# Attention logits as whole-array one-pass products: query parts stacked on the rows, keys doubled and split

## The chip, the core and the metric

The kernel runs on one core of a Trainium2 chip. A core has a matrix engine (TensorE, PE in the profile, with its weight loads shown apart as PEld), a vector engine (VectorE, DVE), a scalar engine with activation functions (ScalarE, ACT), a general engine (GpSimd, POOL) and a queue that issues transfers (SyncE, SP). Each works through its own instructions in order; they wait for one another by semaphores. The metric is the device time of one execution in microseconds, as the median of several.

## What is computed

Two layers of a sequence encoder on 512 tokens of width 1024. Layer 0 mixes tokens by differential attention, layer 1 by gated linear attention; both also attend to 256 memory tokens and end with a gated MLP. The change touches the differential attention of layer 0: six heads, each with two maps of logits (m = 0, 1) of width 64.

```
q = rms_norm(q, qk_norm_g[0]) * (d ** -0.5)        # d = 64
k = rms_norm(k, qk_norm_g[1])
...
logits = einsum('bhmqd,bhmkd->bhmqk', qb, k) + bias
logits = where(visible, logits, -inf)               # chunks of 64 tokens
p = softmax(logits, axis=-1)
w = p[:, :, 0] - lam * p[:, :, 1]
o = einsum('bhqk,bhkv->bhqv', w, v)
```

The heads' outputs are normalised, put beside the memory attention's and sent through the output projection.

## The kernel before

**Number formats.** Everything is held in 32 bits. A product of two F32 operands is issued by `mm` as two records in the profile. Where that is to be avoided, an operand is split into a part `hi`, rounded to the shorter format F32R, and the rest `lo`, also F32R; the large products are sums of three F32R products (hi hi, hi lo, lo hi: L249 to L251 for token-major results, L266 to L268 for feature-major ones). `split` (L231) makes `hi` on ACT and `lo` on DVE; `split_weights` (L198) does so for weights, piece by piece, as they arrive from memory.

**Order.** TensorE runs its instructions exactly as they are written (`manual_schedule`); the other engines' instructions are ordered by the framework when the program is built. So that TensorE has something to do while a softmax is on its way, the independent projections stand in a list, `Filler` (L88): each unit has a cost in us (a quarter of a 128-token block of a projection, six matmuls, counts 6 x 512 / 2370 = 1.296; a unit of output projection, three matmuls, 0.65), and `F.fill(us)` emits units until its credit is used. `F.need(name)` emits all up to a mark.

**Layer 0** (`diff_layer`, L543). The first projection of queries and keys (for heads 0 and 1) is computed at the start; `norms` normalises each 64-column group of the queries, then of the keys (`group_norm`, L298: squares on ACT, sums on DVE, a reciprocal root with one Newton step, a multiplication of 1024 columns on DVE). Then the projection for values and memory queries goes into the filler list, `F.fill(10.0)` emits eight units of it, and `prepare(0)`, one more unit, `prepare(1)` follow. `prepare(h)` (L570) turns the head's 128 columns of queries (both maps) with four TensorE transposes into a PSUM bank, evacuates them on ACT with the gain, and does the same for the keys; so map 0 lies on rows 0 to 63 and map 1 on rows 64 to 127.

A loop of 28 steps follows. Step t emits: `logits(t)` for block t of 24 (head t // 4, 128 queries, 128 (t % 4 + 1) keys); `values(t - 2)`; a fill; at t = 5, 6, 13, 14 `norms` of the next pair of heads (queries at 5 and 13, keys at 6 and 14); `turn(t - 1)`, which transposes the softmax weights; a slot of the memory attention (from t = 12; it turns and multiplies its own blocks); a second fill; at t = 7, 8, 15, 16 `prepare` of heads 2, 3, 4, 5; at t = 7, 11, 15, ... `finish`, which turns a finished head and splits it for the output projection. The fills are 3.0 us each up to t = 13 and 1.2 us after. The filler holds the projections of heads 2 and 3, the memory keys of layer 0, the values, the projection of heads 4 and 5, the memory keys of layer 1, and from t = 14, 20 and 24 on three parts of the output projection (16, 16 and 8 units). What is left is flushed behind the loop; then the last part of the output projection runs.

`logits(u)` (L586) takes two banks of the PSUM ring `lg`, one per map, and for each of two halves of the keys issues one F32 product per map, on 64 rows each. PSUM has four rings of two banks: `mm`, `sm`, `lg` and `tp`; every transpose goes to `tp`, the memory attention's logits to `lg` too.

Of the kernel before, what the change touches and what calls it, by code (L numbers as in the profile page):

```python
# [9 lines left out]
F32 = mybir.dt.float32  # L10
# [117 lines left out]
def trunk(ctx, tc, x_t, mem_t, wpack, cols_a_d, cols_d, conv_d, gate_d, rel_bias, diff_lambda, consts, onehot, out):  # L128
# [169 lines left out]
    def group_norm(pool, y, nb, ng, d, on_dve=False):  # L298
        ss = small("ss")
        for b in range(0, nb, 2):  # L300
            sq = xtile()[:, :2 * ng * d]
            A.activation(sq, y[:, b:b + 2].rearrange("p b n -> p (b n)"), AF.Square)
            V.reduce_sum(ss[:, b * ng:(b + 2) * ng], sq.rearrange("p (g d) -> p g d", d=d), axis=AX.X)
        r = rsqrt(ss[:, :nb * ng], nb * ng, 1.0 / d, on_dve)
        yv = y.rearrange("p b (g d) -> p (b g) d", d=d)
        V.tensor_mul(yv, yv, r.unsqueeze(2).to_broadcast([128, nb * ng, d]))
# [122 lines left out]
    def mem_kv(l):  # L429
# [27 lines left out]
        F.add(0.0, lambda: group_norm(None, km[0], 2, 4, 64))  # L457
# [4 lines left out]
    class MemAttn:  # L462
# [4 lines left out]
        def norm(self):  # L467
            group_norm(self.pool, self.qm, NB, 4, 64, self.on_dve)
# [74 lines left out]
    def diff_layer(pool, mix):  # L543
# [13 lines left out]

        def project_qk(pr):
            qk[pr] = (pool.tile([128, NB, 256], F32, name="qs", bufs=1),
                      pool.tile([128, NB, 256], F32, name="ks", bufs=1))  # L560
            gemm(xh, xl, NB, ("qk", pr), 512, halves(*qk[pr]))
# [8 lines left out]
        def prepare(h):  # L570
            pr, j = divmod(h, 2)
            t2 = []
            for src, g, nm in zip(qk[pr], (c_dq, c_dk), ("qT", "kT")):
                dst = pool.tile([128, S], F32, name=nm, bufs=3)
                p = bank("tp")
                for b in range(NB):
                    transpose(p[:, blk(b)], src[:, b, blk(j)])
                A.activation(dst, p, AF.Copy, scale=g)
                t2.append(dst)
            sm = cp.tile([128, 16], F32, name="smd", tag="smd")  # L580
            heads[h] = dict(q=t2[0], k=t2[1], s2=sm.rearrange("p (m b) -> p m b", b=8),
                            nm=small("nmd"), rc=small("rcd"), v=vs[pr], j=j)
# [3 lines left out]
        def logits(u):  # L586
# [11 lines left out]
            cuts = (0, nk) if i == 0 else (0, nk // 2, nk)  # L598
            for k0, k1 in zip(cuts, cuts[1:]):
                for m in range(2):  # L600
                    hh = blk(m, 64)
                    mm(pls[m][:, k0:k1], H["q"][hh, blk(i)], H["k"][hh, k0:k1], start=True, stop=True)
# [27 lines left out]
        def values(u):  # L630
# [8 lines left out]
            if i == 3:  # L639
# [5 lines left out]
                group_norm(pool, o, NB, 1, 128)  # L645

        def finish(h):
            p = bank("tp")
            for b in range(NB):
# [5 lines left out]
        qk[0] = (pool.tile([128, NB, 256], F32, name="qs", bufs=1),  # L655
                 pool.tile([128, NB, 256], F32, name="ks", bufs=1))
        ev = halves(*qk[0])
# [6 lines left out]
        F.fill(10.0)  # L664
        prepare(0)
        F.fill(1.2)
        prepare(1)
        ma = MemAttn(pool, 0, qm, mix, False)
        M0 = 12
        for t in range(28):  # L670
# [37 lines left out]
            if t in (7, 8, 15, 16):  # L708
                prepare(2 * (t // 7) + (t + 1) % 8)
# [5 lines left out]
    def gla_layer(pool, mix, acc):  # L715
# [199 lines left out]
        for h in range(4):  # L915
# [16 lines left out]
            group_norm(pool, o_[h], NB, 1, 192, True)  # L932
# [204 lines left out]
```

## Time and profile before

| | |
|---|---|
| median of 3 runs | 1207.43 us (1206.88 to 1207.71) |
| the profiled execution | 1206.7 us |
| its span, first to last instruction | 1204.9 us |
| mean granted TensorE clock | 1.000 |
| layer 0's loop, logits first to last | 44.1 to 227.3 us |

In the profile, a line such as `L602 PE MATMUL ps_lg<-kT,qT 64*128 64x128 f32 x72 | 8.4, 308 | ...` is a group of instructions: source line, engine, operation, what is written from what, shape of the weights and of the operand, count, busy time in us and mean of one in ns, and then the idle time of the engine just before them with what ended it. F32R operands are shown as f32 on PE and as fp32r where ACT and DVE write them. A line of the timeline begins with its start and its length in us; several equal instructions in a row are one line with a count. A busy share of TensorE counts pipelined matmuls, so what a matmul costs is read from the distance between starts.

### The profile page before, as it was taken

How to read it: one execution, taken by the hardware profiler on the slowest of the kernel's cores; microseconds unless marked ns; L12 is line 12 of the kernel's file. 1: busy time of each engine (PE TensorE's matmuls, PEld its weight loads, DVE VectorE, ACT ScalarE, POOL GpSimd, SP SyncE). 2: the span in 40 equal slices, each digit the busy share in tenths (PEclk: the TensorE clock that was granted, in tenths of full speed). 3: DMA queues.
4: the chain of work that ended last, by engine and by line, in shares of the span. 5: the costliest groups of instructions: out<-in, count | busy, mean ns of one | idle time of the engine just before them, and what ended most of it. 6: DMA issues, size and time to landing. Idle time of an engine off the chain costs nothing.

```text
span 1204.9 us, 14764 instructions
## 1 busy us (share of the span) xinstructions
PE 1191.4 (99%) x5678; PEld 974.2 (81%) x5678; DVE 758.8 (63%) x1257; ACT 539.7 (45%) x913; POOL 22.9 (2%) x35
## 2 busy tenths in 40 slices
PE   9999999999999999999999999999999999999998
PEld 6887877778888888888787888987888888888887
DVE  7566578887776434767546446768777653476741
ACT  6666666554444222434436444436444432243420
POOL 0000000000000000000110000003000000000000
PEclk9999999999999999999999999999999999999999
DMA  8322231232332331322341221133223233142231
GB/s 291 123 96 80 79 123 45 70 108 85 104 106 70 123 105 57 135 71 88 124 153 59 70 70 58 60 129 128 83 93 117 70 122 93 67 125 83 88 114 44
DMA packets 39376, 117.74 MB, mean 98 GB/s; under 512 B 4685, under 2 KB 5732, under 8 KB 39306
## 3 DMA queue, kind: packets, MB, share of 16 engines
q1 hardware_dynamic: 39162, 116.79, 30.0%
q8 instruction: 44, 0.72, 0.2%
q14 instruction: 26, 0.21, 0.1%
q10 hardware_dynamic: 144, 0.02, 0.0%
HBM read 112.58 MB, written 4.21 MB: 97 GB/s over the span
## 4 chain that ended last, share of the span: by engine, by line
PE 92%; DVE 4%; ACT 2%; issue 1%; DMA 1%; ACTq 0%; DVEq 0%
PE ps_mm L266 8%; PE ps_mm L267 8%; PE ps_mm L268 8%; PE ps_sm L266 6%; PE ps_sm L267 6%; PE ps_sm L268 6%; PE ps_mm L249 6%; PE ps_mm L251 6%; PE ps_mm L250 6%; PE ps_tp L266 3%; PE ps_tp L267 3%; PE ps_tp L268 3%; PE ps_lg L267 3%; PE ps_lg L268 3%; PE ps_lg L266 3%; PE ps_tp L168 2%
## 5 line engine op out<-in xcount | busy, mean ns | idle before, releaser
L199 ACT CAST whi<-raw 128x1024 fp32r<-128x1024 f32 (+4 forms) x215 | 208.4, 974 | 246.7 <-PE ps_tp L267 133.8
L200 DVE TENSOR_TENSOR wlo<-raw,whi 128x1024 fp32r<-128x1024 f32 (+4 forms) x215 | 241.5, 1133 | 110.4 <-ACT whi L199 109.4
L266 PE MATMUL ps_mm<-xsh,whi 128*128 128x512 f32 x480 | 190.7, 397 | 2.0 <-DVE xt L950 2.0
L267 PE MATMUL ps_mm<-xsl,whi 128*128 128x512 f32 x480 | 187.1, 390 | 0.1
L268 PE MATMUL ps_mm<-xsh,wlo 128*128 128x512 f32 x480 | 187.1, 390 | 0.0
L249 PE MATMUL ps_mm<-whi,xsh 128*128 128x512 f32 (+2 forms) x352 | 138.6, 394 | 0.0
L266 PE MATMUL ps_sm<-xsh,whi 128*128 128x512 f32 x352 | 136.9, 389 | 0.0
L267 PE MATMUL ps_sm<-xsl,whi 128*128 128x512 f32 x352 | 136.9, 389 | 0.0
L268 PE MATMUL ps_sm<-xsh,wlo 128*128 128x512 f32 x352 | 136.9, 389 | 0.0
L251 PE MATMUL ps_mm<-whi,xsl 128*128 128x512 f32 (+2 forms) x352 | 131.3, 373 | 0.3 <-DVE xsl L233 0.3
L250 PE MATMUL ps_mm<-wlo,xsh 128*128 128x512 f32 (+2 forms) x352 | 130.6, 371 | 0.0
L999 ACT ACTIVATE cvo<-u,cv 128x512 f32<-128x512 f32 x88 | 71.6, 814 | 113.9 <-DVE u L997 113.5
L266 PEld LDWEIGHTS ps_mm<-xsh,whi 128*128 128x128 f32 x480 | 90.2, 188 | 22.2 <-DVE xt L950 2.4
L268 PEld LDWEIGHTS ps_mm<-xsh,wlo 128*128 128x128 f32 x480 | 90.1, 188 | 19.1
L267 PEld LDWEIGHTS ps_mm<-xsl,whi 128*128 128x128 f32 x480 | 90.2, 188 | 18.8 <-DVE xsl L233 0.8
L1000 DVE SCALAR_TENSOR_TENSOR cvo<-u,cv,cvo 128x512 f32<-128x512 f32 x88 | 65.9, 749 | 31.6 <-ACT cvo L999 31.4
L249 PEld LDWEIGHTS ps_mm<-whi,xsh 128*128 128x128 f32 x352 | 66.3, 188 | 13.8 <-issue 3.2
L268 PEld LDWEIGHTS ps_sm<-xsh,wlo 128*128 128x128 f32 x352 | 66.1, 188 | 13.8
L266 PEld LDWEIGHTS ps_sm<-xsh,whi 128*128 128x128 f32 x352 | 66.1, 188 | 13.7
L267 PEld LDWEIGHTS ps_sm<-xsl,whi 128*128 128x128 f32 x352 | 66.1, 188 | 13.6
L251 PEld LDWEIGHTS ps_mm<-whi,xsl 128*128 128x128 f32 x352 | 66.1, 188 | 12.7 <-DVE xsl L233 0.5
L250 PEld LDWEIGHTS ps_mm<-wlo,xsh 128*128 128x128 f32 x352 | 66.5, 189 | 9.3
(238 smaller groups left out, 1766.9 us busy)
## 6 DMA issues: line engine op xcount, KB each, us to landing
raw<-in_wpack_dram SPq DMA_DIRECT2D x176, 512.0 KB, 3.6
raw<-in_wpack_dram SPq DMA_DIRECT2D x28, 256.0 KB, 2.8
xt<-in_x_t_dram SPq DMA_DIRECT2D x16, 256.0 KB, 4.9
xres<-xt SPq DMA_DIRECT2D x8, 256.0 KB, 2.0
xt<-xres SPq DMA_DIRECT2D x8, 256.0 KB, 3.7
out_dram<-xt SPq DMA_DIRECT2D x8, 256.0 KB, 2.0
bt<-bias_d SPq DMA_DIRECT2D x6, 256.0 KB, 5.5
raw<-in_wpack_dram SPq DMA_DIRECT2D x4, 384.0 KB, 2.9
```

What stands on the lines that cost most here:

```text
L168: nc.tensor.transpose(dst, src, ident[:n, :n])
L199: A.copy(hi[:, c], raw[:, c])
L200: V.tensor_sub(lo[:, c], raw[:, c], hi[:, c].bitcast(F32))
L249: mm(p, sh[k][:, blk(b)], hi, start=k == 0, stop=False)
L250: mm(p, sh[k][:, blk(b)], lo, start=False, stop=False)
L251: mm(p, sl[k][:, blk(b)], hi, start=False, stop=k == KT - 1)
L266: mm(p, hi[:, blk(n)], bh, start=i == first, stop=False)
L267: mm(p, hi[:, blk(n)], bl, start=False, stop=False)
L268: mm(p, lo[:, blk(n)], bh, start=False, stop=i == last)
L999: A.activation(c, u[:, 2:], AF.Identity, scale=cv[l][:, 2, j:j + 1], bias=cv[l][:, 3, j:j + 1])
L1000: V.scalar_tensor_tensor(c, u[:, 1:S + 1], cv[l][:, 1, j:j + 1], c, op0=ALU.mult, op1=ALU.add)
```

## The change

Queries and keys are held with room for two copies of each 64-column group: `doubles()` makes tiles of [128, 4, 4, 2, 64]. After the norm the queries' second copy becomes their value rounded to F32R (ACT) and the first the rest (a subtraction on DVE); the keys' second copy is a plain copy (ACT). A transposed map then has 128 rows: 64 of the queries' rest and 64 of the rounded queries, and the keys twice. Both gains go to the keys (`c_dk` is multiplied by `c_dq` once). `prepare(h, m)` works on one map: four transposes and a copy of the queries into F32R, four transposes of the keys and a split into `kh` and `kl`. `logits` issues, per map, one F32R product with `kh` and one with `kl` over all keys, 128 rows deep, into the same bank.

The order changes with it: 12.5 us of filler instead of 10 ahead of the first preparation, a fill of 1.2 behind each of the four preparations there, and in the loop the first map is prepared ahead of `turn`, the second where the head was prepared before. `group_norm` takes its groups as one dimension, which is only another way of writing it for most callers; for the memory keys it makes two halves of 256 columns instead of one of 512.

```diff
-    def group_norm(pool, y, nb, ng, d, on_dve=False):
+    def group_norm(y, d, on_dve=False):
+        n = y.shape[1]
         ss = small("ss")
...
+        for h in (slice(0, n // 2), slice(n // 2, n)):
+            sq = xtile()[:, :n // 2 * d].rearrange("p (g d) -> p g d", d=d)
+            A.activation(sq, y[:, h], AF.Square)
+            V.reduce_sum(ss[:, h], sq, axis=AX.X)
+        r = rsqrt(ss[:, :n], n, 1.0 / d, on_dve)
+        V.tensor_mul(y, y, r.unsqueeze(2).to_broadcast([128, n, d]))
...
+        V.tensor_mul(c_dk, c_dk, c_dq)
...
+        def doubles():
+            return [pool.tile([128, NB, 4, 2, 64], F32, name=n, bufs=1) for n in ("qs", "ks")]
+
+        def ev_qk(q, k):
+            def ev(b, p):
+                for d, c in ((q, p[:, :256]), (k, p[:, 256:])):
+                    A.activation(d[:, b, :, 0], c.rearrange("p (g d) -> p g d", d=64), AF.Copy, scale=r[:, b:b + 1])
+            return ev
...
         def norms(pr, i):
             F.need(f"qk{pr}")
-            group_norm(pool, qk[pr][i], NB, 4, 64)
+            y = qk[pr][i].rearrange("p b g t d -> p (b g) t d")
+            group_norm(y[:, :, 0], 64)
+            if i:
+                A.copy(y[:, :, 1], y[:, :, 0])
+            else:
+                A.copy(y[:, :, 1].bitcast(F32R), y[:, :, 0])
+                V.tensor_sub(y[:, :, 0], y[:, :, 0], y[:, :, 1])
...
+        def prepare(h, m):
             pr, j = divmod(h, 2)
...
+            q, k = (t[:, :, 2 * j + m].rearrange("p b t d -> p b (t d)") for t in qk[pr])
+            p = bank("tp")
+            for b in range(NB):
+                transpose(p[:, blk(b)], q[:, b])
+            H["q", m] = pool.tile([128, S], F32R, name=f"qT{m}", bufs=2)
+            A.copy(H["q", m], p)
+            p = bank("tp")
+            for b in range(NB):
+                transpose(p[:, blk(b)], k[:, b])
+            H["kh", m] = pool.tile([128, S], F32R, name=f"kh{m}", bufs=2)
+            H["kl", m] = pool.tile([128, S], F32R, name=f"kl{m}", bufs=2)
+            split(H["kh", m], H["kl", m], p, c_dk)
...
-            cuts = (0, nk) if i == 0 else (0, nk // 2, nk)
-            for k0, k1 in zip(cuts, cuts[1:]):
-                for m in range(2):
-                    hh = blk(m, 64)
-                    mm(pls[m][:, k0:k1], H["q"][hh, blk(i)], H["k"][hh, k0:k1], start=True, stop=True)
+            for m in range(2):
+                for part in ("kh", "kl"):
+                    mm(pls[m][:, :nk], H["q", m][:, blk(i)], H[part, m][:, :nk], start=part == "kh",
+                       stop=part == "kl")
...
-        F.fill(10.0)
-        prepare(0)
-        F.fill(1.2)
-        prepare(1)
+        F.fill(12.5)
+        for h in range(2):
+            for m in range(2):
+                prepare(h, m)
+                F.fill(1.2)
...
+            ahead = 2 * (t // 7) + (t + 1) % 8 if t in (7, 8, 15, 16) else None
+            if ahead:
+                prepare(ahead, 0)
             if 0 <= t - 1 < 24:
                 turn(t - 1)
             ma.slot(t - M0)
             F.fill(f)
-            if t in (7, 8, 15, 16):
-                prepare(2 * (t // 7) + (t + 1) % 8)
+            if ahead:
+                prepare(ahead, 1)
```

More of the change, by code (lines that the diff above doesn't have):

```diff
@@ L295, in trunk, with groups @@
     c_go = lambda t: col(23 + t)
-    def group_norm(pool, y, nb, ng, d, on_dve=False):
+    def group_norm(y, d, on_dve=False):
+        n = y.shape[1]
         ss = small("ss")
[L300 to L306, printed above, removed]
+        for h in (slice(0, n // 2), slice(n // 2, n)):
[4 more added lines that the diff above has]
+        V.tensor_mul(y, y, r.unsqueeze(2).to_broadcast([128, n, d]))
+    def groups(y, d):
+        return y.rearrange("p b (g d) -> p (b g) d", d=d)
     def bias_rows(rb, oh, bs):
@@ L567, in norms @@
             F.need(f"qk{pr}")
-            group_norm(pool, qk[pr][i], NB, 4, 64)
-        def prepare(h):
-            pr, j = divmod(h, 2)
[L572 to L582, printed above, removed]
+            y = qk[pr][i].rearrange("p b g t d -> p (b g) t d")
[6 more added lines that the diff above has]
+        def prepare(h, m):
+            pr, j = divmod(h, 2)
+            if m == 0:
+                sm = cp.tile([128, 16], F32, name="smd", tag="smd")
+                heads[h] = dict(s2=sm.rearrange("p (m b) -> p m b", b=8), nm=small("nmd"), rc=small("rcd"),
+                                v=vs[pr], j=j)
+            H = heads[h]
+            q, k = (t[:, :, 2 * j + m].rearrange("p b t d -> p b (t d)") for t in qk[pr])
[10 more added lines that the diff above has]
+            split(H["kh", m], H["kl", m], p, c_dk)
         live = {}
```

18 lines of the change are left out of this document (8 added, 10 removed).

## The prediction

> **What bounds the kernel now.** I read the page's busy shares and chain of waits first, then busy time by stretch, then TensorE instruction by instruction.
>
> ```profile
> PE 1191.4 (99%) x5678; PEld 974.2 (81%) x5678; DVE 758.8 (63%) x1257; ACT 539.7 (45%) x913; POOL 22.9 (2%) x35
> ...
> PE 92%; DVE 4%; ACT 2%; issue 1%; DMA 1%; ACTq 0%; DVEq 0%
> ```
>
> ```profile
> 44.00:215.00 171.00, 167.58 (x942) 133.70 (x941) 118.34 (x316) 109.43 (x276) 0.58 (x4) 1.00 0.28 87
> 215.00:260.00 45.00, 43.13 (x227) 34.00 (x226) 38.65 (x79) 23.79 (x48) 0.20 (x4) 1.00 0.26 82
> ```
>
> The columns after the length are PE, PEld, DVE, ACT and POOL busy time, the granted clock, DMA share and GB/s. TensorE is the bound throughout, in a fixed order, so time changes by what its own stream loses or gains and by each place where it waits. In the stretch that the change touches (44 to 215 us) DVE is busy 69% and ACT 64%: room on average, none to be sure of at a given moment.
>
> The logits (L602) are issued as f32 products on 64 rows, each as two records:
>
> ```profile
> L602 PE MATMUL ps_lg<-kT,qT 64*128 64x128 f32 x72 | 8.4, 308 | 1.0 <-ACT kmT L454 0.6 <-ACT xt L492 0.3
> ...
> L602 PE MATMUL ps_lg<-kT,qT 64*128 64x256 f32 x48 | 8.2, 406 | 0.6 <-ACT xt L492 0.5
> ```
>
> Busy time hides their price; the order of starts shows it. Three blocks, for 256, 512 and 128 keys, with what stands around them:
>
> ```profile
> 51.21 0.39 PE L251 MATMUL ps_mm<-whi,xsl 128*128 128x512 f32 x1
> 51.52 0.72 PE L602 MATMUL ps_lg<-kT,qT 64*128 64x128 f32 x8
> 52.17 0.50 PE L249 MATMUL ps_mm<-whi,xsh 128*128 128x512 f32 x1
> 52.51 0.39 PE L250 MATMUL ps_mm<-wlo,xsh 128*128 128x512 f32 x1
> ...
> 66.07 0.39 PE L251 MATMUL ps_mm<-whi,xsl 128*128 128x512 f32 x1
> 66.39 1.14 PE L602 MATMUL ps_lg<-kT,qT 64*128 64x256 f32 x8
> 67.45 0.71 PE L638 MATMUL ps_sm<-v,xt 128*128 128x128 f32 x4
> 67.92 0.48 PE L249 MATMUL ps_mm<-whi,xsh 128*128 128x512 f32 x1
> 68.23 0.39 PE L250 MATMUL ps_mm<-wlo,xsh 128*128 128x512 f32 x1
> 68.47 0.40 PE L251 MATMUL ps_mm<-whi,xsl 128*128 128x512 f32 x1
> ...
> 74.97 0.39 PE L251 MATMUL ps_mm<-whi,xsl 128*128 128x512 f32 x1
> 75.29 0.49 PE L602 MATMUL ps_lg<-kT,qT 64*128 64x128 f32 x4
> 75.71 0.94 PE L638 MATMUL ps_sm<-v,xt 128*128 128x128 f32 x6
> 76.72 0.39 PE L250 MATMUL ps_mm<-wlo,xsh 128*128 128x512 f32 x1
> ```
>
> Undisturbed projection products start 0.23 us apart (68.23, then 68.47). So 256 keys cost 52.51 - 51.21 - 2 x 0.23 = 0.84 us of the stream. With the value products (L638) taken out at 0.11 us each (the row of eight in the last fence: 1.05 us, less one 0.27 us tail, over seven), 512 keys cost 2.16 - 0.46 - 0.44 = 1.26, 128 keys 1.75 - 0.46 - 0.67 = 0.62. That is 0.21 us per 128 keys and 0.41 us whatever the size; 384 keys, on the same line, cost 1.05. The 0.41 lies before and behind the block (0.31 from L251 to L602 instead of 0.23, 0.34 from L249 to L250), and the f32 value products, on all 128 rows, show none of it: it belongs to going to half the rows and back.
>
> **The change part by part.** *Products (A).* Four one-pass products per block, 128 rows deep, replace them. Priced as the projections' products, 512 keys take 4 x 0.23 = 0.91. A width of 256 is in the trace, in the second layer:
>
> ```profile
> 772.62 0.28 PE L249 MATMUL ps_mm<-whi,xsh 128*128 128x256 f32 x1
> 772.74 0.28 PE L250 MATMUL ps_mm<-wlo,xsh 128*128 128x256 f32 x1
> ```
>
> 0.12 us each: 0.48 for 256 keys, and 0.70 for 384 by the line between. One-pass products 128 wide don't occur. The lower end is the same line carried on (0.065 each); the upper is the old rate, 0.21. I take 0.11, that of the nearest rows of this width (value products and transposes), since a weight load goes with each: 0.45. A head then costs 0.45 + 0.48 + 0.70 + 0.91 = 2.54 instead of 0.62 + 0.84 + 1.05 + 1.26 = 3.77; six heads save 7.4 us. [...]
>
> Against that stand transposes: sixteen a head for eight, 48 more. Four of q and then four of k:
>
> ```profile
> 180.38 0.60 PE L168 MATMUL ps_tp<-C,qs 128*128 128x128 f32 x4
> 180.81 0.60 PE L168 MATMUL ps_tp<-C,ks 128*128 128x128 f32 x4
> 181.84 0.66 PE L168 MATMUL ps_tp<-C,o 128*128 128x128 f32 x4 [0.42 <-ACT qT L578]
> ```
>
> 180.38 to 180.81 is four: 0.108 each, 5.2 us. **A = -2.2 us** (-3.3 to +0.2 by the ends of the 128-wide price).
>
> *ACT and DVE.* The durations:
>
> ```profile
> L199 ACT CAST whi<-raw 128x1024 fp32r<-128x1024 f32 x19 | 20.0, 1051 | 4.5 <-PE ps_mm L251 4.1 <-DMA raw<-in_wpack_dram 0.4
> ...
> L578 ACT ACTIVATE kT<-ps_tp,cols 128x512 f32<-128x512 f32 x6 | 4.1, 687 | 0.0
> ...
> L627 ACT COPY xt<-ps_tp 128x512 f32<-128x512 f32 x4 | 2.3, 581 | 0.0
> ```
>
> ```profile
> L306 DVE TENSOR_TENSOR qs<-qs,rs_y 128x1024 f32<-128x1024 f32 x2 | 2.5, 1225 | 0.1
> ...
> L233 DVE SCALAR_TENSOR_TENSOR xsl<-ps_tp,cols,xsh 128x512 fp32r<-128x512 f32 x3 | 2.3, 751 | 10.8 <-ACT xsh L232 10.8
> ```
>
> ACT: six copies of 1024 columns (6.3 us), and twelve q copies (0.58) plus twelve upper key parts (0.69) instead of twelve at 0.69: +13.3 us. DVE: three subtractions of 1024 (3.7) and twelve lower key parts (9.0): +12.7 us. Over 171 us ACT goes to 72% and DVE to 77%. Under TensorE's stream that is free; it costs where TensorE stands right behind it. The strided evacuations keep their element counts, and I cost them, the 64-column halves of the memory keys' norm and the one tiny product of gains at nothing: all lie under projections; uncovered they are under 0.5 us together.
>
> *Transpose banks (D, C, G).* The row above at 181.84 shows what a third user of the two transpose banks pays: from 180.81 four transposes end at 181.24, it starts at 181.84, 0.6 us late. The change moves the first half of each preparation ahead of `turn`, making `turn` the third user, at t = 7, 8 and 16 (at 15 a longer wait hides it). A copy is 0.1 shorter than the old evacuation: **D = 3 x 0.5 = +1.5 us** (0.6 to 3). On the other hand this wait
>
> ```profile
> 189.61 0.66 PE L168 MATMUL ps_tp<-C,ks 128*128 128x128 f32 x4 [1.08 <-DVE xt L502]
> ```
>
> arises because nothing stood between the memory attention's `turn` and `prepare` (the filler gave no unit there at t = 16); now two units of output projection (1.4 us) do: **C = -1.1** (-1.1 to 0). At the start, keys wait for the bank of the previous keys, freed by ACT and then DVE, about as long as one filler unit lasts: **G = +0.3** (0 to 1.5). The later start of the first preparation (12.5 instead of 10 us of filler) covers the longer norm: the copy and subtraction add about 2.3 us, two filler units 2.8.
>
> *Logit banks (B).* TensorE also waits for the memory attention to free the logit banks:
>
> ```profile
> PEld ps_lg L602 <- ACT xt L492: 2.7, 5, 0.7
> ...
> PEld ps_lg L602 <- ACT kmT L454: 1.4, 2, 0.8
> ```
>
> ```profile
> 173.47 0.70 PE L602 MATMUL ps_lg<-kT,qT 64*128 64x256 f32 x2 [0.24 <-ACT xt L492]
> 174.38 1.13 PE L602 MATMUL ps_lg<-kT,qT 64*128 64x256 f32 x6 [0.21 <-ACT xt L492]
> 175.44 0.71 PE L638 MATMUL ps_sm<-v,xt 128*128 128x128 f32 x4
> ```
>
> Here the second map waits when only the first two of the block's eight records have run. The new order does both products of map 0 first: at 512 keys the block would go on 0.45 us after the second bank is free instead of 1.06. Over the seven waits I take **B = -1.3** (-2 to +1: a stream that comes earlier waits longer).
>
> *Waits that the change adds (E, H).* `prepare` moves from the end of step 15 to ahead of `turn`, and now wants the keys doubled:
>
> ```profile
> 177.78 1.20 DVE L306 TENSOR_TENSOR ks<-ks,rs_y 128x1024 f32<-128x1024 f32 x1
> ```
>
> Before, the keys were wanted at 180.81 and ready at 178.98. Now a copy (1.05) and a hand-over (0.15) make it 180.2, while TensorE gets there at 175.44 + 0.44 (values) + 0.69 (one unit of output projection, see F) + 0.43 (queries) = 177.0. Everything in step 15 is queued behind it on TensorE: `turn`, the memory attention, fillers. Gap 3.2 us; part of DVE's queue ahead of 177.78 moves up with TensorE. **E = +2.6** (0, if the norm is ordered earlier, to 4.4, with the new subtraction ahead of it on DVE). At t = 7 the same meets a lighter DVE, because its filler work is done a step earlier; I cost it at nothing, 1.3 at worst. **H**: at t = 7 and 15 the second map's keys are split right before logits that need them: hi 0.69 and lo 0.75 in a row behind a q copy end 2.85 us after the first q transpose, TensorE wants them at 2.15: 2 x 0.7 = **+1.4** (0 to 3).
>
> *Filler (F).* Counting the list's own costs (1.296 per projection unit, 0.65 per output unit): before, 9 units are spent ahead of step 0, after it 14. Behind them stand 71 units (92 us) and 40 output units (26), against 14 x 6 + 14 x 2.4 = 117.6 us asked for: it just lasts. Now 66 are left, and it runs dry at t = 19 and from the middle of t = 26. The last norm loses its cover:
>
> ```profile
> 236.54 1.05 PE L638 MATMUL ps_sm<-v,xt 128*128 128x128 f32 x8
> ...
> 243.28 0.69 DVE L306 TENSOR_TENSOR o<-o,rs_y 128x512 f32<-128x512 f32 x1
> 244.93 0.60 PE L168 MATMUL ps_tp<-C,o 128*128 128x128 f32 x4
> ```
>
> Values end at 237.4, the result is ready at 243.97, transposes wait for it. Ten units lay between; five are left, 3.4 us. The chain takes 6.6, of which some 3.2 us is other DVE work that partly goes away: **F = +1.5** (0 to 3.2).
>
> Sum: A -2.2, B -1.3, C -1.1, D +1.5, E +2.6, F +1.5, G +0.3, H +1.4 = **+2.7 us**. The profiled execution took 1206.7 us (span 1204.9, 1.8 around it); the median shown is 1207.43, 0.7 above it. On the median: **1210.1 us**.
>
> **The rivals.** *R1, not slower: the added work is covered.* DVE and ACT get to the norm and the splits in time, E, F, G and H are 0: -2.2 - 1.3 - 1.1 + 1.5 = -3.1, 1204.3 us. For it: the second projection of queries and keys ends a step earlier, and DVE is idle for 31% of the stretch. Against: the keys' norm was ready only 1.8 us before its use. It decides at step 15: if the doubled keys are there when TensorE arrives. *R2, only E vanishes*: +0.1, 1207.5. *R3, DVE is late at every key split*: one split (0.75) at each of twelve, 9.0 instead of G + H = 1.7: +10.0, 1217.4. It needs DVE over 90% busy there; the stretch has 69%, but 215 to 260 us has 86%. *R4, the change doesn't do what it says*: the 0.41 us per block isn't bound to half rows and stays: 24 x 0.41 = 9.8 more, 1219.9. Against it stand the value products. [...]
>
> **How the numbers follow.** Forecast 0.43, R1 0.27, R2 0.18, R3 0.07, R4 0.05. A measurement of this kernel can tell about 0.2%, 2.4 us: 1205.0 to 1209.8 is no change. The forecast's own range is 1208.3 to 1213, a third of it within; R1 is nearly all faster, R2 within, the rest slower: faster 0.25, same 0.34, slower 0.41. The range, 1203.5 to 1215.0, takes in R1, R2, the ends of A and most of E, F, H; R3 and R4 lie outside.
>
> **What would show it.** A: logit blocks of four records, four sizes near 0.45, 0.48, 0.70, 0.91 us, and no 0.31 and 0.34 us steps around them. E: an idle step at the key transposes near 175 us, released by ACT. D and H: 0.5 us steps at `turn` and at the logits of heads 2 and 4. F: a wait of the last `o` transposes for DVE. No waits there means R1. It is wrong as a whole if 128-wide one-pass products take 0.2 us, or if waits appear at every preparation.

## The result and the profile after

The changed kernel takes 1215.41 us (1212.85 to 1217.66, 4 runs); the kernel before took 1207.35 on the same chip. The ratio is 1.0066 (95% interval 1.0054 to 1.0078): slower by 8 us. The forecast was 1210.1 with a range of 1203.5 to 1215.0, so the sign was right and the size 5.3 us short. The profiled execution took 1216.42 us (span 1214.6) against 1206.7 (span 1204.9), 9.7 more. Engines and chain on the page of after:

```profile
PE 1194.1 (98%) x5654; PEld 984.2 (81%) x5654; DVE 770.2 (63%) x1275; ACT 553.3 (46%) x933; POOL 22.9 (2%) x35
...
PE 91%; DVE 5%; ACT 2%; issue 1%; DMA 0%; POOL 0%; ACTq 0%; DVEq 0%; POOLq 0%
```

TensorE has 24 instructions fewer, DVE 11 us and ACT 14 us more (12.7 and 13.3 were worked out). That alone explains no loss: TensorE is the bound. So the question is where its stream stands still. First, in which part of the program: the first product of layer 0's MLP, in the order of instructions (start, duration) of before and then of after:

```profile
268.83 1.02 PE L1006 MATMUL ps_tp<-xt,C 128*128 128x512 f32 x2
```

```profile
278.58 1.02 PE L1036 MATMUL ps_tp<-xt,C 128*128 128x512 f32 x2
```

From there to the end it is 1204.9 - 268.8 = 936.1 us before and 1214.6 - 278.6 = 936.0 after. All 9.75 us are lost ahead of it, in the layer that the change touches.

Next, the products themselves. TensorE's order of instructions in after, a block of 128 keys between projection products, and half a block of 512:

```profile
52.97 0.40 PE L251 MATMUL ps_mm<-whi,xsl 128*128 128x512 f32 x1
53.20 0.22 PE L628 MATMUL ps_lg<-kh,qT 128*128 128x128 f32 x1
...
53.48 0.28 PE L628 MATMUL ps_lg<-kl,qT 128*128 128x128 f32 x1
53.60 0.44 PE L249 MATMUL ps_mm<-whi,xsh 128*128 128x512 f32 x1
...
105.80 0.39 PE L628 MATMUL ps_lg<-kh,qT 128*128 128x512 f32 x1
106.03 0.39 PE L628 MATMUL ps_lg<-kl,qT 128*128 128x512 f32 x1
```

From L251 to L628 it is the 0.23 us of any projection product: the step of 0.31 is gone. Products over 512 keys start 0.23 apart, 0.91 a block. Counted as the forecast counts, from the L251 ahead of a block to the L250 behind it, undisturbed blocks cost 0.45, 0.47, 0.71 and 0.91 us for 128, 256, 384 and 512 keys, against 0.45, 0.48, 0.70 and 0.91 forecast. The products do what was forecast. The loss is in these places (last column: the wait ahead of the instruction, and what released it):

```profile
112.48 0.66 PE L168 MATMUL ps_tp<-C,ks 128*128 128x128 f32 x4 [0.30 <-ACT ks L585]
...
118.77 0.33 PE L628 MATMUL ps_lg<-kl,qT 128*128 128x128 f32 x1 [0.43 <-DVE kl L233]
...
122.85 0.60 PE L168 MATMUL ps_tp<-C,ks 128*128 128x128 f32 x4
124.20 0.55 PE L168 MATMUL ps_tp<-C,xt 128*128 128x128 f32 x3 [0.74 <-ACT qT L604]
...
175.83 1.00 PE L518 MATMUL ps_sm<-vm,xt 128*128 128x64 f32 x8
177.79 1.61 PE L489 MATMUL ps_lg<-kmT,xt 64*128 64x256 f32 x8 [0.96 <-DVE nmd L634]
...
184.16 0.60 PE L168 MATMUL ps_tp<-C,qs 128*128 128x128 f32 x4
187.08 0.65 PE L168 MATMUL ps_tp<-C,ks 128*128 128x128 f32 x4 [2.32 <-ACT ks L585]
...
248.91 0.39 PE L268 MATMUL ps_mm<-xsh,wlo 128*128 128x512 f32 x1
252.35 1.09 PE L168 MATMUL ps_tp<-C,o 128*128 128x128 f32 x4 [3.06 <-DVE o L306]
...
254.52 0.63 PE L266 MATMUL ps_mm<-xsh,whi 128*128 128x512 f32 x1
254.94 0.63 PE L267 MATMUL ps_mm<-xsl,whi 128*128 128x512 f32 x1
...
258.46 0.40 PE L267 MATMUL ps_mm<-xsl,whi 128*128 128x512 f32 x1
258.69 0.40 PE L268 MATMUL ps_mm<-xsh,wlo 128*128 128x512 f32 x1
```

The reader is to see, in this order: the doubled keys late at step 7 and at step 15 (E); the low part of map 1's keys late (H, at step 8, and once more at step 16); `turn` behind the copy of q (D); the memory logits of step 14 behind the softmax's maxima, which no term of the forecast had; and the last norm without cover (F). What counts for the time is start to start: 187.08 - 184.16 = 2.92, less 0.43 for four transposes, is 2.5 us. The last four rows are something else: nothing waits, but at 254.5 products start 0.42 us apart, at 258.5 again 0.23. Busy time and granted clock by stretch in after (length; PE, PEld, DVE, ACT, POOL busy; PEclk; DMA share; GB/s) say why:

```profile
176.20:179.60 3.40, 2.44 (x16) 1.74 (x16) 3.19 (x7) 2.89 (x9) 0.00 (x0) 0.99 0.32 100
179.60:183.00 3.40, 3.40 (x11) 2.78 (x10) 3.40 (x11) 3.40 (x14) 0.00 (x0) 0.50 0.00 0
183.00:186.40 3.40, 1.76 (x12) 1.32 (x10) 3.40 (x13) 2.22 (x7) 0.00 (x0) 1.00 0.00 0
247.80:251.20 3.40, 1.49 (x7) 0.91 (x5) 3.27 (x9) 1.55 (x3) 0.00 (x0) 1.00 0.54 154
251.20:254.60 3.40, 2.25 (x8) 1.99 (x9) 1.38 (x4) 0.69 (x1) 0.20 (x4) 0.51 0.47 154
254.60:258.00 3.40, 3.40 (x10) 2.63 (x9) 0.35 (x1) 0.00 (x0) 0.00 (x0) 0.50 0.00 0
```

Three stretches of 3.41 us run at half clock, one at step 14 and two behind the last norm, each behind a stretch in which TensorE was busy for 2.44 us or less. The clock record of the kernel before has none up to the end of its span. By the granted 0.50, an estimate: one fully busy stretch at half clock costs half of itself, 1.7 us; here the first costs 1.7 and the other two, busy from 252.35 on, (258.0 - 252.35) / 2 = 2.8: 4.5 us in all.

The theory to be tested: A holds; the loss is a number of single waits, each with a place and a cause in the order of the work, and half clock behind some of them. Its rival: ACT and DVE, given 13 us more each, are short of time over the whole stretch, so that a wait taken away at one place turns up at another.

### The profile page after: what moved, and what is told of

The parts are those of the page before. It is cut to its first block, busy times and chain, and to the rows that moved or that the text cites. A ratio compares the mean times of both kernels' runs of the same rounds, so it can differ in the third digit from the quotient of the medians.

```text
span 1214.6 us, 14754 instructions
## 1 busy us (share of the span) xinstructions
PE 1194.1 (98%) x5654; PEld 984.2 (81%) x5654; DVE 770.2 (63%) x1275; ACT 553.3 (46%) x933; POOL 22.9 (2%) x35
## 4 chain that ended last, share of the span: by engine, by line
PE 91%; DVE 5%; ACT 2%; issue 1%; DMA 0%; POOL 0%; ACTq 0%; DVEq 0%; POOLq 0%
PE ps_mm L266 9%; PE ps_mm L267 9%; PE ps_mm L268 9%; PE ps_sm L268 6%; PE ps_sm L267 6%; PE ps_sm L266 6%; PE ps_mm L249 5%; PE ps_mm L251 5%; PE ps_mm L250 5%; PE ps_tp L266 3%; PE ps_tp L267 3%; PE ps_tp L268 3%; PE ps_lg L267 3%; PE ps_lg L268 3%; PE ps_lg L266 3%; PE ps_tp L168 3%
## 5 line engine op out<-in xcount | busy, mean ns | idle before, releaser
L251 PE MATMUL ps_mm<-whi,xsl 128*128 128x512 f32 (+2 forms) x352 | 131.3, 373 | 0.3 <-DVE xsl L233 0.3
L250 PE MATMUL ps_mm<-wlo,xsh 128*128 128x512 f32 (+2 forms) x352 | 130.6, 371 | 0.0
L251 PEld LDWEIGHTS ps_mm<-whi,xsl 128*128 128x128 f32 x352 | 66.2, 188 | 12.7 <-DVE xsl L233 0.5
L250 PEld LDWEIGHTS ps_mm<-wlo,xsh 128*128 128x128 f32 x352 | 66.5, 189 | 9.4
```

Of the source, the lines that this page charges most:

```text
L250: mm(p, sh[k][:, blk(b)], lo, start=False, stop=False)
L251: mm(p, sl[k][:, blk(b)], hi, start=False, stop=k == KT - 1)
```

## The experiments

Twelve kernels ran. Each time stands beside runs of the kernel before on the same chip (medians 1206.94 to 1207.59).

**The order without the products.** Two kernels have the products of before. The first has only the filler moved ahead:

```
-        F.fill(10.0)
-        prepare(0)
-        F.fill(1.2)
-        prepare(1)
+        F.fill(12.5)
+        for h in range(2):
+            prepare(h)
+            F.fill(1.2)
+            F.fill(1.2)
```

> The kernel before, old logits, with only the filler order of the change: 12.5 us of filler and four fills of 1.2 around its two preparations, 14 units spent ahead instead of 9. Theory (dry filler): the last o transposes wait for DVE by 2 to 3.5 us, with or without a stretch at half clock behind, 1207.4 + 3 to 6 = 1210 to 1213. Rival (the new ACT and DVE work makes that wait): under 0.5 us of wait there, 1207 to 1208.

The second has the whole order of the change, with q as the first half of a preparation and k as the second:

```
...
+            ahead = 2 * (t // 7) + (t + 1) % 8 if t in (7, 8, 15, 16) else None
+            if ahead:
+                prepare(ahead, 0)
             if 0 <= t - 1 < 24:
                 turn(t - 1)
             ma.slot(t - M0)
             F.fill(f)
-            if t in (7, 8, 15, 16):
-                prepare(2 * (t // 7) + (t + 1) % 8)
+            if ahead:
+                prepare(ahead, 1)
```

> The kernel of before (its products, its single queries and keys) in the order of the change: 12.5 us of filler ahead, a unit behind each half of a preparation (queries, keys), and at steps 7, 8, 15, 16 the queries ahead of the step's transposes and the keys at its end. Theory (the order costs what the empty list costs, 3.3 by the earlier run, and 0.4 at each of three steps as third user of the transpose banks, and saves the 1.1 at step 16): 1207.4 + 3.3 + 1.2 - 1.1 = 1210.8. If so, the rest of the change's loss of 8, some 4.6, is the products' and the doubling's although the products alone save. Rival (the order carries all of the loss): 1214 or more.

Measured: 1210.65 us, ratio 1.0026 (1.0016 to 1.0037), and 1210.73, 1.0032 (1.0020 to 1.0044). The order of the filler, which leaves the list empty at the end of the loop, costs 3.3 us by itself, and the rest of the order next to nothing with the old products. Both have the same wait before the last norm's transposes; TensorE's rows of the first and then of the second:

```profile
247.79 0.63 PE L168 MATMUL ps_tp<-C,o 128*128 128x128 f32 x4 [3.06 <-DVE o L306]
...
248.49 0.40 PE L267 MATMUL ps_mm<-xsl,whi 128*128 128x512 f32 x1
248.72 0.39 PE L268 MATMUL ps_mm<-xsh,wlo 128*128 128x512 f32 x1
```

```profile
247.73 0.63 PE L168 MATMUL ps_tp<-C,o 128*128 128x128 f32 x4 [3.06 <-DVE o L306]
...
248.50 0.63 PE L267 MATMUL ps_mm<-xsl,whi 128*128 128x512 f32 x1
248.93 0.63 PE L268 MATMUL ps_mm<-xsh,wlo 128*128 128x512 f32 x1
```

The wait is the same, 3.06 us; behind it the one runs at full clock (0.23 apart) and the other at half (0.43). From these transposes to the MLP the first takes 271.27 - 247.79 = 23.48 us and the second 272.86 - 247.73 = 25.13. So the half clock is no part of the wait and has its own price, 1.65 us for one stretch; and it isn't certain. In after the same way takes 278.58 - 252.35 = 26.23, with two stretches.

**The filler made to last.** After, with less filler in each half of steps 0 to 13:

```
-FA, FB = 3.0, 1.2
+FA, FB = 2.78, 1.2
```

> The changed kernel with fills of 2.78 instead of 3.0 us in steps 0 to 13, so that the filler list, which starts five units ahead, lasts to the end of the loop. Theory (the dry filler costs the last norm its cover, and the long wait halves the TensorE clock): the 3.1 us wait of the last o transposes falls under 0.5 us and the 6.8 us at half clock behind it go, 3.2 + 2.3 = 5.5 us less, about 1210. Rival (the wait only moves, since five units less stand in steps 0 to 13): waits of as much in all appear at the earlier steps, 1214 to 1217.

Measured: 1215.90, 1.0072 (1.0057 to 1.0087). F's wait is gone and nothing is won. TensorE's rows of this run:

```profile
111.33 0.90 PE L168 MATMUL ps_tp<-C,ks 128*128 128x128 f32 x3 [2.51 <-ACT ks L585]
...
177.05 1.27 PE L489 MATMUL ps_lg<-kmT,xt 64*128 64x256 f32 x3 [3.41 <-DVE nmd L634]
```

By the last column TensorE waits 2.51 us for the keys of step 7 (0.30 in after) and 3.41 for the memory logits of step 14 (0.96). Half clock is as long as in after, three stretches. Here the rival won: by the places of the new waits, 0.22 us of filler less in each half step was cover that the norms needed.

**The norms a step earlier.** After, with

```
-            if t in (5, 6, 13, 14):
-                norms((t + 3) // 8, (t + 3) % 8)
+            if t in (4, 5, 12, 13):
+                norms((t + 4) // 8, (t + 4) % 8)
```

> The changed kernel with the four norms of queries and keys emitted one step earlier (t = 4, 5, 12, 13). Theory (the keys' norm and its copy are late at step 15): the waits for the doubled keys, 2.3 us at t = 15 and 0.3 at t = 7, go, about 2.6 us less, 1212.8, and the last o wait stays at 3.1 us. Rival (DVE is simply full there): the wait at the key transposes is replaced by later ones on DVE of the same length, 1215.

Measured: 1213.06, 1.0045 (1.0028 to 1.0061), 2.4 us less than after. E's waits at steps 7 and 15 are gone, and with them the one at step 14; F's 3.2 stays. But new waits have come, the longest at the logits of step 15:

```profile
180.65 0.50 PE L628 MATMUL ps_lg<-kh,qT 128*128 128x512 f32 x1 [1.16 <-ACT xt L496]
```

Counted as in the table further below and without slow steps at half clock, the waits of the profiled run add up to 14.8 us, and those of after to 14.9: in length they only moved, as the rival said. What this run saves is clock: it has one stretch at half clock (250.51 to 253.92) where after has three. So the keys' wait has its cause in the order, since it goes when the norm is moved; that there is room for the added work isn't shown by this run.

**Keeping the array busy ahead of the last norm.** After, with three products of constants ahead of the last transposes, which nothing reads:

```
+        def warm(n):
+            p = bank("lg")
+            for _ in range(n):
+                mm(p, C[:, 512:640], C[:, 0:512], start=True, stop=True)
...
+            if t == 27:
+                warm(3)
             if t % 4 == 3 and t >= 7:
                 finish(t // 4 - 1)
```

> The changed kernel with three idle f32 products of constants, 128 by 512 (six records, some 2.6 us of TensorE) ahead of the last o transposes, where it waits 3.1 us. They compute nothing that is used. Theory (the clock is halved because TensorE stands still): the o transposes start when they did, but the products behind them are 0.23 us apart instead of 0.43, 2.0 to 2.5 us less than the changed kernel. Rival (the clock falls for the load, or at random): no gain, the stretch at half clock stays or moves, 0 to +1 us.

Measured: 1215.53, 1.0067 (1.0052 to 1.0082): no gain in the median. In its profile (1216.18) the way from the last transposes to the MLP is 277.42 - 253.94 = 23.48, as in the run without half clock, 2.75 less than in after. But that run starts its first preparation about 1 us later than after and takes 0.9 more from the MLP on, which neither kernel nor theory accounts for, and had one stretch at half clock elsewhere (188.34 to 191.76). The price of the half clock is confirmed; keeping the array busy with empty products as a remedy is not.

**The new products in the old order.** After, with the start and the preparations of before:

```
-        F.fill(12.5)
-        for h in range(2):
-            for m in range(2):
-                prepare(h, m)
-                F.fill(1.2)
+        F.fill(10.0)
+        prepare(0, 0)
+        prepare(0, 1)
+        F.fill(1.2)
+        prepare(1, 0)
+        prepare(1, 1)
...
-            if ahead:
-                prepare(ahead, 1)
+            if t in (7, 8, 15, 16):
+                for m in range(2):
+                    prepare(2 * (t // 7) + (t + 1) % 8, m)
```

> New products and doubled keys, but the order of before: 10 us of filler ahead of the first preparation, one filler unit between the two heads, both maps of a preparation in a row at the end of steps 7, 8, 15 and 16. Theory (the new order was needed and is not the source of the loss; the products gain 3.5 us): the wait for o goes (-3.2) and the list lasts, but four banks of transposes in a row wait for the splits of map 0 (1.2 us at each preparation) and the logits at steps 8 and 16 wait for the split of map 1 (1.2 more each), and the first preparation waits 2 us for the longer norm: 1207.4 - 3.5 + 7.2 + 4 = about 1215. Rival (the loss is the order's, that is the 14 units spent ahead and the halves put ahead of the step's transposes): no such waits, 1207.4 - 3.5 = 1204 to 1206.

Measured: 1219.10, 1.0097 (1.0082 to 1.0112), the slowest of all. With four banks in a row (TensorE's rows of this run) the second queries wait for the bank of the first, the second keys for that of the first keys, and the logits for the second split. (The profile names `qT` for the wait of the keys, but what ends just before them, at 113.45, is the low part of the first keys' split on DVE.)

```profile
112.13 0.66 PE L168 MATMUL ps_tp<-C,qs 128*128 128x128 f32 x4 [0.24 <-ACT qT L604]
113.47 0.66 PE L168 MATMUL ps_tp<-C,ks 128*128 128x128 f32 x4 [0.68 <-ACT qT L604]
...
115.69 0.33 PE L628 MATMUL ps_lg<-kl,qT 128*128 128x128 f32 x1 [0.46 <-DVE kl L233]
```

So the new order wasn't what made the change slow; without it, it is slower by 3.7.

**Both long waits at once.** After, with the norms a step earlier and FB = 0.98 instead of 1.2, so that the list lasts without taking from steps 0 to 13:

> The changed kernel with norms a step earlier (as e2, 1213.1) and filler of 0.98 instead of 1.2 us from step 14 on, so that units are left at steps 26 and 27 beside the last norm. Theory (the two long waits are independent): the 3.2 us wait for o goes and with it the half clock behind it (1.7): 1213.1 - 4.0 = about 1209. Rival (with less filler in steps 14 to 23 the same time comes back as waits for the softmax there): 1212 to 1214, with waits of 3 us in all behind DVE between steps 14 and 23 that e2 doesn't have.

Measured: 1209.86, 1.0020 (1.0010 to 1.0029), 3.2 less than with the norms moved alone. F's wait is gone and nothing of its length has come instead (11.1 us of waits, 14.8 without the lasting list). With both edits 5.5 of the 8 us are won back. A wait of 1.45 us at the memory logits of step 14, with one stretch at half clock behind it, is left.

**Spreading the rest, three times with a new wait.** Three kernels move the halves of preparations apart. The first has the norms as above, FB = 1.07, 11 units of filler ahead of step 0, head 1 prepared within steps 0 and 1, and this order (`mid` ahead of `turn`, `last` at the end of a step):

```
+            mid = {7: (2, 1), 8: (3, 0), 15: (4, 1)}
+            last = {0: (1, 0), 1: (1, 1), 6: (2, 0), 8: (3, 1), 14: (4, 0), 15: (5, 0), 16: (5, 1)}
```

> The changed kernel with its halves spread out: norms a step earlier (steps 4, 5, 12, 13), head 1 prepared within steps 0 and 1 instead of ahead of them (10 units ahead instead of 14), head 2 at the end of step 6 and in step 7, head 4 at the end of step 14 and in step 15, head 5 at the ends of steps 15 and 16, filler of 1.07 instead of 1.2 us from step 14 on so that the list lasts. Theory (products are worth -3.5 and the loss is the sum of single waits, each with its place, plus half clock behind the two long ones): waits for keys, for o and for the splits of heads 2 and 4 go, some 1.5 us of bank waits stay: 1207.4 - 3.5 + 1.5 = 1205.4. Rival (ACT and DVE are short of time over the whole stretch, so waits only move): new waits of 4 us or more between steps 5 and 23, 1209 or more.

The second has 12 units ahead and cuts each preparation of heads 1 to 5 in four, keys first, at the head of a step (ahead of its filler), in its middle (ahead of `turn`) or at its end, and issues the doubling copy at the end of the norm's step; the full filler lasts to step 14, and FB is 0.92. By step, with (head, map, part):

```
head of step:   {1: (1, 1, "k"), 2: (1, 1, "q"), 6: (2, 0, "k"), 7: (2, 0, "q"), 8: (3, 0, "k"),
                 9: (3, 1, "q"), 14: (4, 0, "k"), 15: (4, 0, "q"), 16: (5, 0, "k"), 17: (5, 0, "q")}
middle of step: {8: (3, 1, "k")}
end of step:    {0: (1, 0, "k"), 1: (1, 0, "q"), 6: (2, 1, "k"), 7: (2, 1, "q"), 8: (3, 0, "q"),
                 14: (4, 1, "k"), 15: (4, 1, "q"), 16: (5, 1, "k"), 17: (5, 1, "q")}
norms (pr, i):  {4: (1, 1), 5: (1, 0), 12: (2, 1), 13: (2, 0)}
```

> The changed kernel with each preparation cut in four (keys and queries of each map by themselves, keys first), one quarter at a time with filler between it and the next user of the transpose banks; norms a step earlier, keys ahead of queries, and the doubling copy issued at the end of the norm's step, behind the copy that the step's own transposes need on ACT; 12 units ahead; full filler up to step 14 and 0.92 us from step 15. Beside the run with norms earlier and the list lasting (1209.9): theory (each wait has its own place and cause) takes away six bank waits of 0.4 to 1.1 (3.7 in all), two waits for the split of map 1 (1.2), the memory logits' wait of 1.6 at step 14 with the half clock behind it (1.7): 1209.9 - 8.2 = about 1202 at best, 1204 if a third of it stays. Rival (ACT and DVE have no room, so single waits move to other places): 1208 to 1212 with new waits of 4 us or more.

The third is the second with another engine for one operation:

```
-                V.tensor_sub(y[:, :, 0], y[:, :, 0], y[:, :, 1])
+                G.tensor_sub(y[:, :, 0], y[:, :, 0], y[:, :, 1])
```

> As the run with quarters, with the three query subtractions of 1024 columns on GpSimd instead of DVE. If DVE's queue is what still makes waits (the maxima behind a norm), it is 1 to 2 us faster than the run with quarters; if the waits there come from the order on ACT, or if GpSimd takes over 3 us for it and the queries come late, the same within 0.5 us or slower.

Measured: 1213.01 (1.0034 to 1.0064 around 1.0049), 1214.58 (1.0052 to 1.0088 around 1.0070) and 1212.96 (1.0032 to 1.0062 around 1.0047). By the times the rival won the first two, the second being slower than even its rival's 1208 to 1212; the third is 1.6 us faster than the second, as expected if DVE's queue still made waits. By the traces, the waits that were to go did go: in the third, no transposes for `turn` wait for a copy of q, and no logits for a split. What came instead is mainly one wait of about 4 us, at step 6, in all three, with one stretch at half clock behind it; TensorE and then ACT in the third:

```profile
97.42 0.33 PE L634 MATMUL ps_lg<-kl,qT 128*128 128x384 f32 x1
101.73 0.49 PE L671 MATMUL ps_sm<-v,xt 128*128 128x128 f32 x2 [3.98 <-ACT xt L660]
```

```profile
98.71 1.04 ACT L199 CAST whi<-raw 128x1024 fp32r<-128x1024 f32 x1 [1.92 <-DMA raw<-in_wpack_dram]
...
101.42 0.26 ACT L660 COPY xt<-ps_tp 128x128 f32<-128x128 f32 x1
```

The values of step 6 want the copy that ACT makes for `turn`, and in ACT's order a weight cast stands ahead of it, which waited 1.92 us for its load. In the first of the three it stands at the memory's evacuation, for the token factors from DVE. Both belong to the projection of the memory, which with 11 or 12 units ahead of step 0 instead of 14 falls just ahead of that copy. By this reading it isn't lack of room but which two things meet; the next kernel tests it.

**The same with 14 units ahead.** The third of these with the start of the change (12.5 and four times 1.2 us of filler), quarters for heads 2 to 5 only, and FB = 0.98:

> The run with norms earlier and the list lasting (1209.9: 14 units ahead, 3.0 and 0.98 us of filler, so the memory's projection keeps the place in which its weights come in time), with the quarters for heads 2 to 5, the doubling copies at the end of the norm's step and the query subtractions on GpSimd. Theory: the 4 us wait at step 6 of the runs with quarters came from 12 units ahead instead of 14 (a weight cast on ACT waits for its load and holds the copy that the step's transposes need), so it goes here, and the six bank waits (3.7), two waits for the split of map 1 (1.2) and most of the 1.6 at step 14 with the half clock behind it go too: 1209.9 - 7 = about 1203, faster than before by 0.3%. Rival (waits only move): 1207 to 1211.

Measured: 1206.45 (11 runs), 0.9996 (0.9987 to 1.0005). The wait at step 6 is gone, and the kernel is level with the one before. (The preparation of head 1 and the filler from step 14 on differ too, so the 14 units weren't tried alone.) Two waits were left that have a plain cause, 1.05 at the queries of step 7 (the GpSimd subtraction takes 2.46 us, 1.22 on DVE) and 1.45 at the memory logits of step 14, so:

```
-FA, FB = 3.0, 0.98
+FA, FB = 3.0, 0.9
-            f = FA if t < 14 else FB
+            f = FA if t < 14 else 2.0 if t == 14 else FB
-                G.tensor_sub(y[:, :, 0], y[:, :, 0], y[:, :, 1])
+                (G if pr == 2 else V).tensor_sub(y[:, :, 0], y[:, :, 0], y[:, :, 1])
```

> The run with quarters and a lasting list (1206.45), with filler of 2.0 us in each half of step 14 and 0.9 from step 15 on, and the first of the two query subtractions in the loop back on DVE (on GpSimd it takes 2.46 us and TensorE waited 1.05 for it). Theory: a unit of 1.3 us goes between the values and the memory logits of step 14, whose wait of 1.45 goes to 0.2; with the 1.05 that makes 1206.45 - 2.3 = 1204.2, 0.25% faster than before. Rival (the time comes back): the logits of steps 18 to 22 wait longer for the memory attention's reads of the logit banks because their steps have 0.08 us less filler a half, and the one subtraction pushes other work on DVE back: 1206 to 1207.5.

Measured: **1204.88 us** (1204.25 to 1205.48, 11 runs) against 1207.59, ratio 0.9978 (0.9969 to 0.9987): faster than both kernels. At step 14 the memory logits follow the values without a wait:

```profile
175.30 1.00 PE L518 MATMUL ps_sm<-vm,xt 128*128 128x64 f32 x8
176.23 1.58 PE L489 MATMUL ps_lg<-kmT,xt 64*128 64x256 f32 x8
```

## Why the prediction missed, point by point

The sizes are start-to-start steps of TensorE: from the step between two starts the usual one is taken off (0.23 for 512 columns, 0.12 for 256, 0.11 for 128 and for transposes), and what is over 0.25 us counts as a wait. From the end of the first projection to the MLP, such waits make 7.4 us before, 15.5 in after (0.7 of it slow steps at half clock) and 7.1 in the last kernel.

| term | forecast | profiled run of after |
|---|---|---|
| A, products and transposes | -2.2 | -2.15 (below) |
| B, logit banks | -1.3 | -1.1, but +1.1 at step 14: 0 |
| C, wait of step 16 | -1.1 | -1.25 |
| D, `turn` third | +1.5 | +1.3, and -0.3 at `finish` |
| E, doubled keys | +2.6 | +2.5, and +0.5 at step 7 |
| F, last norm | +1.5 | +3.2 |
| G, start | +0.3 | +0.3 |
| H, split of map 1 | +1.4 | +1.35 |
| other single waits | 0 | -0.2 |
| sum of terms | +2.7 | +5.2 |
| half clock | not in it | +4.5 |

- **A was right.** The blocks have the prices forecast (0.45, 0.47, 0.71, 0.91). The sum is best read from the last kernel, which has the products and all 48 transposes, nearly the waits of before and no half clock in this part: from the first projection's end to the MLP it takes 236.59 us, before 239.09. Less the waits, 229.50 and 231.65: 2.15 us saved. R4 is out with it. One reading behind A was too strong: the value products do show a slower step behind them, 0.31 instead of 0.23 (67.92 to 68.23 in the forecast's own rows), and so do value products and transposes in after. So up to 0.08 of the 0.41 us isn't due to half the rows alone; where it stands in both kernels it changes nothing in the difference.
- **C, D, E, G and H were right in place, and in size within 0.5 us.** E's cause was shown by moving the norm, which took the wait at the keys away (though not its length from the sum of waits), D's and H's by the quarters, which removed both. The hand-over of 0.15 us in E's working was an estimate that no row shows: in after the doubling copy ends at 187.03 (186.00 + 1.03) and the transposes start at 187.08, 0.05 later.
- **B failed in part.** The logits wait less, but the banks have a third customer: the memory logits of step 14 want a bank that the softmax's maxima on DVE (L634) must free, and these stand behind the query norm and its new subtraction (L588). The forecast named "a stream that comes earlier waits longer" as B's upper end and didn't look for whose wait that would be. This term was 1.3 us short.
- **F failed in size.** Its working had the chain of 6.6 us and a cover of 3.4, and then took 1.5, the middle, because "some 3.2 us is other DVE work that partly goes away". It doesn't. DVE in after:

```profile
245.89 0.69 DVE L670 TENSOR_TENSOR o<-ps_sm,rs 128x512 f32<-128x512 f32 x1 [0.71 <-PE ps_sm L665]
246.58 0.69 DVE L980 TENSOR_TENSOR xt<-xt,ps_mm 128x512 f32<-128x512 f32 x1
...
250.18 1.23 DVE L200 TENSOR_TENSOR wlo<-raw,whi 128x1024 fp32r<-128x1024 f32 x1
...
251.51 0.69 DVE L306 TENSOR_TENSOR o<-o,rs_y 128x512 f32<-128x512 f32 x1
```

  From 245.89 to 252.20 DVE is as long at it as before, 6.3 us. The residual additions and weight splits belong to output units issued earlier and to weights of the next, which nothing withdrew. The upper end, 3.2, was the value that the forecast's own rows gave, and the kernel with only the filler moved ahead has the same wait, 3.06 us, with the old products.
- **The step that decided: a wait was priced as its own length.** The sum has no term for the clock behind a wait, and no reason is given for putting it at nothing. With the terms at their measured sizes the kernel would stand 5.2 above before, at about 1212.6, and its fastest run, at a mean granted clock of 0.999, is at 1212.85 (another at 0.999 took 1214.40). The two runs at 0.995, the profiled one among them, took 1216.42 and 1217.66. What separates them goes with the half clock behind waits, 4.5 us in the profiled run. So of the 5.3 us that the median is off, 2.5 are mis-sized terms (F +1.7 and B +1.3 above all) and the other 2.8 lie in what the sum left out. The forecast had looked at the granted clock only in before, where it is 1.00 in that part, and no row there shows a long wait. The trace of after has stretches of 3.41 and 6.83 us at 0.50, whose starts, 179.56 and 251.24, lie 71.68 = 21 x 3.413 us apart.
- **The rivals.** R1 (the work is covered, 1204.3) is what the last kernel comes to, 1204.88, but only in another order. This is also what decides between single waits and a lack of room on ACT and DVE: with the same added work but for one subtraction moved to GpSimd, its waits (7.1 us) are no longer than before the change (7.4). The products of before weren't run in that order. R2 is out, since E came in full. R3's sign, DVE late at every split, isn't seen: two of twelve made TensorE wait by more than 0.3 us.

What stays open: the last kernel still has waits of 1.4 us at a `finish` (230.8) and 0.7 at the logits of step 19 (205.8), which weren't tried; and the two unexplained losses of the kernel with the empty products.

## What to carry to other kernels

Work that is "free" on an engine off the bound is free only at the moments when nothing stands right behind it (here 2.5 us were lost at the doubled keys of step 15, with ACT busy for 46% of the span and DVE for 63%): before adding to a norm or a split, write down for each consumer how long before its use the result was ready, and move the producer by as much as is added. Filler is a budget: what is spent ahead of a loop is missing at its end, where the last chain has no other cover, and taking it from the middle uncovers other chains. Price a wait of TensorE with what comes behind it: where it may be busy for 1.5 us or less of a stretch of 3.41 us, which half clock followed each time here, add up to 1.7 us (1.65 measured for one stretch), and look for units of real work to put there. And when a wait is taken away, add up all waits of the new trace: here one edit only moved them and still gained, by the clock.

## What the hardware showed

In these runs the clock didn't follow the length of a single wait. In all fourteen records it changes only at borders 3.413 us apart that run on through an execution: in after at 179.56, 182.97, 251.24, 258.07 and 1213.80 us, with 1, 20, 2 and 280 such lengths between them. At `o`, the two kernels with the products of before have the same wait of 3.06 us, and a border falls at another place in it. Busy time by such stretches, in the one that kept its clock (borders counted back from its last microseconds, which run at half clock) and then in the one that lost it:

```profile
243.15:246.56 3.41, 1.58 (x7) 0.95 (x6) 3.28 (x9) 1.55 (x3) 0.00 (x0) 1.00 0.49 154
246.56:249.97 3.41, 2.18 (x12) 1.93 (x13) 1.80 (x4) 0.69 (x1) 0.20 (x4) 1.00 0.46 154
```

```profile
244.90:248.30 3.40, 0.57 (x5) 0.60 (x6) 2.56 (x5) 0.62 (x1) 0.00 (x0) 1.00 0.45 159
248.30:251.70 3.40, 3.40 (x10) 2.65 (x9) 0.75 (x1) 0.69 (x1) 0.20 (x4) 0.50 0.33 136
```

In the first the wait is shared by two stretches, each with TensorE busy for 1.58 us or more, and costs no clock. In the second it fills most of one, and the next is at half. In after, the 2.5 us wait at step 15 cost none (1.76 busy in 183.00 to 186.40), while 1.49 busy in 247.80 to 251.20 did, and so did step 14 with a wait of only 1.1 us and 2.44 busy, in a stretch otherwise filled mostly by products of 64 rows or 64 columns. By these rows 1.9 us idle (3.40 - 1.49) within one stretch were enough. The wait at step 15 makes the same point as the one at `o`: it is 2.32 us both in after and in the kernel with the empty products, but there it falls into one stretch, and the next ran at half clock:

```profile
184.93:188.34 3.41, 1.09 (x11) 1.06 (x11) 3.41 (x12) 3.31 (x7) 0.00 (x0) 1.00 0.11 19
```

Away from both ends of an execution, the fourteen traces here have ten stretches at full clock with TensorE busy for 1.5 us or less (1.47 at most when cut exactly at the borders), and half clock followed each of them. Of those with 1.57 or more only two were followed by it, both at step 14 (2.45 in after, 2.0 in the kernel with both long waits removed). Whether the small products of step 14 have a part in it was not tried. One execution of each kernel was profiled, so that the borders fall elsewhere in another execution of the same kernel isn't shown; it would go with the mean clocks of after's runs, 0.995 and 0.999, and their spread over 4.8 us, while the runs of the last kernel, with no wait over 1.5, lie within 1.3.
